# Cross-covariance attention: V loaded eight heads at a time, in 8 KB runs

## The chip, the core and the metric

The kernel runs on one core of one Trainium2 chip. A core has five engines that run side by side, each with its own queue of instructions in program order: TensorE (PE; its weight loads are listed apart as PEld), VectorE (DVE), ScalarE (ACT), GpSimd (POOL) and SyncE (SP), which here does nothing but issue transfers. Sixteen DMA engines move data between HBM and the on-chip memory SBUF; matmuls write into PSUM. The metric is the device time of one execution in microseconds.

## What is computed

For each of 8 batches and 12 heads there are Q, K and V of 512 rows by 64 columns, float32. Q and K are divided by the norm of each of their columns, the 64x64 matrix of their products is put through a softmax along its last axis, and V is multiplied by it:

```python
Q_norm = Q / (np.linalg.norm(Q, axis=-2, keepdims=True) + 1e-10)
K_norm = K / (np.linalg.norm(K, axis=-2, keepdims=True) + 1e-10)
attn = np.einsum('bhnd,bhne->bhde', Q_norm, K_norm)
attn = np.exp(attn - np.max(attn, axis=-1, keepdims=True))
attn = attn / (np.sum(attn, axis=-1, keepdims=True) + 1e-10)
out = np.einsum('bhnd,bhde->bhne', V, attn)
```

Inputs are 37.75 MB and the output 12.58 MB.

## The kernel before

The work is cut into 24 units of 4 heads. A unit's Q, K and V are 512 KB each. Each is loaded into a tile of 128 partitions, 32 partitions to a head, with 16 rows of 64 values (4 KB, one contiguous run) in a partition. The output of a unit is stored with two runs of 2 KB in a partition.

What is done for one unit:

- Q and K are cast to bf16 into one tile, side by side (`cast_q` L80, `cast_k` L83, VectorE). 64 matmuls give each head's 128x128 Gram matrix (`grams` L95). Its diagonal holds the squared norms (`norms` L107, VectorE, and a power on GpSimd, L112), its lower left block K against Q, which ScalarE keeps (`keep_kq` L100), GpSimd scales (L117), TensorE transposes (`logits` L123) and VectorE scales (`scale_q` L127). Then come the exponential (`exps` L131, ScalarE) and the division (`normalise` L135 to L139, VectorE), which writes the softmax into a block-diagonal matrix; a matmul and a ScalarE copy place it a second time (`doubled` L165, L166).
- V is cast to bf16 into `vb`, one half on ScalarE and one on VectorE (`cast_v` L88). TensorE transposes eight blocks of 128x128, each with two rows of V in its columns, into one PSUM tile (`vtrans` L145), and one ScalarE copy brings them to SBUF as `vt` (L148). That copy goes in the order of its source: it reads PSUM contiguously and writes every other bf16 element, so that two blocks lie interleaved.
- `outs` (L176) multiplies the transposed V by the block-diagonal softmax, half a unit in each PSUM tile `po`; copies (L180) bring the result to `so`, and `store` (L76) writes it out.

The order is written out by hand; nothing is reordered. Iteration s of the main loop loads Q and K of unit s+3, computes the Gram matrix of unit s, the logits of s-1, and the outputs of units n0 to n1-1, where n1 = `outs_by(s)` is (s-2)*9//10 and at least 0. So outputs fall behind, and at the end 6 of the 24 units are left. V is loaded up to unit n1+3, cast and transposed up to unit n1; the casts stand at the head of the iteration, ahead of `cast_q(s+1)` on VectorE. On TensorE an iteration runs grams, logits, outs, doubled, vtrans. Stores follow three outputs behind. All transfers are issued from SP's queue in that order, and each issue waits until the transfer eight places earlier has landed.

After the loop the Gram matrices' PSUM is free, and the last units' V goes without the cast: `vtrans_f32` (L159, L160) transposes float32 blocks, two PSUM tiles to a unit, and ScalarE and VectorE copy one each. It runs one unit ahead of `outs`. There `outs` has one of its two copies on each engine.

Of the kernel before, what the change touches and what calls it, by code (L numbers as in the profile page):

```python
# [8 lines left out]
F32 = mybir.dt.float32  # L9
BF16 = mybir.dt.bfloat16  # L10
# [4 lines left out]
D = 64  # L15
HU = 4
NV = 32
R = 16
SV = 2
MV = 64  # L20
TP = 4
# [3 lines left out]
def kernel(  # L25
# [7 lines left out]
    nc = tc.nc  # L33
    B, H, N, _ = Q.shape
    assert N == NV * R and Q.shape[3] == D
    U = B * H // HU

    Qf, Kf, Vf = (x.rearrange("b h n d -> (b h n d)").rearrange("(u p f) -> u p f", p=128, f=R * D) for x in (Q, K, V))
    Of = out.rearrange("b h n d -> (b h n d)").rearrange("(u s p f) -> u p s f", s=SV, p=128, f=TP * 2 * D)

    ctx.enter_context(tc.manual_schedule())

    const = ctx.enter_context(tc.tile_pool(name="const", bufs=1))
    qp = ctx.enter_context(tc.tile_pool(name="qp", bufs=5))
    vp = ctx.enter_context(tc.tile_pool(name="vp", bufs=6))
    vbp = ctx.enter_context(tc.tile_pool(name="vbp", bufs=4))
    qkp = ctx.enter_context(tc.tile_pool(name="qkp", bufs=4))
    vtp = ctx.enter_context(tc.tile_pool(name="vtp", bufs=3))
    sop = ctx.enter_context(tc.tile_pool(name="sop", bufs=10))
# [2 lines left out]
    ps_v = ctx.enter_context(tc.tile_pool(name="ps_v", bufs=1, space=bass.MemoryType.PSUM))  # L52
# [5 lines left out]
    def outs_by(s):  # L58

        return max(0, (s - 2) * 9 // 10)  # L60


    qf, kf, vf, vb, qkb, nsq, rq, kqs, sl, ex, vt, so, kq = ({} for _ in range(13))

    def load_qk(u):
        qf[u] = qp.tile([128, R, D], F32, name="qf")
        kf[u] = qp.tile([128, R, D], F32, name="kf")
        nc.sync.dma_start(out=qf[u].rearrange("p t d -> p (t d)"), in_=Qf[u])
        nc.sync.dma_start(out=kf[u].rearrange("p t d -> p (t d)"), in_=Kf[u])

    def load_v(u):
        vf[u] = vp.tile([128, R * D], F32, name="vf")
        nc.sync.dma_start(out=vf[u], in_=Vf[u])

    def store(u, g=slice(0, SV)):
        nc.sync.dma_start(out=Of[u][:, g], in_=so[u][:, g].rearrange("p s t d -> p s (t d)"))  # L76

    def cast_q(u):
        qkb[u] = qkp.tile([128, R, 2 * D], BF16, name="qkb")
        nc.vector.tensor_copy(qkb[u][:, :, 0:D], qf[u])  # L80
# [1 line left out]
    def cast_k(u):  # L82
        nc.vector.tensor_copy(qkb[u][:, :, D:], kf[u])  # L83

    def cast_v(u):
        w = vb[u] = vbp.tile([128, R // 2, 2 * D], BF16, name="vb")
        for half, copy in ((slice(0, TP), nc.scalar.copy), (slice(TP, None), nc.vector.tensor_copy)):
            copy(w[:, half], vf[u].rearrange("p (t d) -> p t d", d=2 * D)[:, half])  # L88

    def grams(u):  # L90

# [29 lines left out]
    def logits(u):  # L121
        for h in range(HU):
            nc.tensor.transpose(lg[:, h, :], kqs[u][D:, h, :], ident[D:, D:])  # L123

    def scale_q(u):
        s = sl[u] = small.tile([D, HU, D], F32, name="sl")
        nc.vector.tensor_tensor(out=s, in0=lg, in1=rq[u][0:D, :, None].to_broadcast([D, HU, D]), op=ALU.mult)  # L127

    def exps(u):
        e = ex[u] = small.tile([D, HU, D], F32, name="ex")  # L130
        nc.scalar.activation(e, sl[u], AF.Exp)  # L131

    def normalise(u):
        s = small.tile([D, HU], F32, name="esum")
        nc.vector.reduce_sum(out=s, in_=ex[u], axis=AX.X)  # L135
        ri = small.tile([D, HU], F32, name="rinv")
        nc.vector.reciprocal(ri, s)
        a = abuf[u % len(abuf)]
        nc.vector.tensor_tensor(out=a[0:D, :, 0, :], in0=ex[u], in1=ri[:, :, None].to_broadcast([D, HU, D]), op=ALU.mult)  # L139

    def vtrans(u):

        ps = ps_v.tile([128, R // 2, 128], BF16, name="vps")
        for t in range(R // 2):
            nc.tensor.transpose(ps[:, t, :], vb[u][:, t, :], identb)  # L145

        w = vt[u] = vtp.tile([128, TP, 128, 2], BF16, name="vt")
        nc.scalar.copy(w.rearrange("p t c a -> p a t c"), ps.rearrange("p (a t) c -> p a t c", a=2))  # L148

    def vtrans_f32(u):  # L150

        w = vt[u] = vtp.tile([128, TP, 128, 2], BF16, name="vt")
        for i in range(2):
            half = slice(i * TP // 2, (i + 1) * TP // 2)
            ps = ps_t.tile([128, TP // 2, 128, 2], F32, name="vps32")
            for t in range(TP // 2):
                for a in range(2):
                    c = (a * TP + i * TP // 2 + t) * 2 * D
                    nc.tensor.transpose(ps[:, t, :, a], vf[u][:, c:c + 2 * D], ident)  # L159
            both[i](w[:, half], ps)  # L160

    def doubled(u):

        a = abuf[u % len(abuf)]
        nc.tensor.matmul(dup[D:], identb[0:D, 0:D], a[0:D, :, 0, :], tile_position=(0, D))  # L165
        nc.scalar.copy(a[D:, :, 1, :], dup[D:])  # L166

    def outs(u, copies=(nc.scalar.copy, nc.scalar.copy)):
        s = so[u] = sop.tile([128, SV, TP, 2 * D], F32, name="so")
        a = abuf[u % len(abuf)]  # L170
        for g in range(SV):
            po = ps_o.tile([128, TP, 2 * D], F32, name="po")
            for t in range(TP):
                for x in range(2):
                    h = 2 * g + x
                    nc.tensor.matmul(  # L176
                        po[MV * x:MV * (x + 1), t, :], vt[u][:, t, NV * h:NV * (h + 1), :].rearrange("p c a -> p (c a)"),
                        a[:, h].rearrange("p a d -> p (a d)"), tile_position=(0, MV * x),
                    )
            copies[g](s[:, g], po)  # L180
# [11 lines left out]
    ident = const.tile([128, 128], F32, name="ident")  # L192
    make_identity(nc, ident)
    identb = const.tile([128, 128], BF16, name="identb")
# [4 lines left out]
    for i in range(12):  # L199
        a = const.tile([128, HU, 2, D], BF16, name=f"ab{i}")  # L200
# [3 lines left out]
    def on(f, u):  # L204
        if 0 <= u < U:
            f(u)

    on(cast_q, 0)
    on(cast_k, 0)
    on(load_v, 0)  # L210
    on(load_v, 1)
    nv, nst, nt = 2, 0, 0
    for s in range(U):
        n0, n1 = outs_by(s - 1), outs_by(s)
        on(load_qk, s + LOAD_AHEAD)
        while nv < min(U, n1 + 4):
            load_v(nv)
            nv += 1
        while nst < n1 - 3:
            store(nst)  # L220
            nst += 1
        new = range(nt, n1 + 1) if s >= 1 else ()
        for v in new:
            cast_v(v)
        on(cast_q, s + 1)
        on(normalise, s - 2)
        on(grams, s)
        on(norms, s)
        on(keep_kq, s)
        on(scale_k, s)  # L230
        on(logits, s - 1)
        on(scale_q, s - 1)
        on(exps, s - 1)
        on(cast_k, s + 1)
        for v in range(n0, n1):
            outs(v)
        on(doubled, s - 2)
        for v in new:
            vtrans(v)
            nt = v + 1  # L240
# [3 lines left out]
    ps_t = ctx.enter_context(tc.tile_pool(name="ps_t", bufs=4, space=bass.MemoryType.PSUM))  # L244
    both = (nc.scalar.copy, nc.vector.tensor_copy)

    for i, u in enumerate(range(n1, U)):
        on(load_v, u + 4)
        store(u - 3)
        if i == 0:  # L250
            normalise(last - 1)
        if i == 2:
            scale_q(last)
            exps(last)
        if i == 3:
            normalise(last)
        on(vtrans_f32, u + 1)
        if i == 1:
            doubled(last - 1)
        if i == 3:  # L260
            doubled(last)
        outs(u, both)
        if i == 1:
            logits(last)
    for u in range(U - 3, last):
        store(u)
    for g in range(SV):
        store(last, slice(g, g + 1))
# [29 lines left out]
```

## Time and profile before

| what | value |
| --- | --- |
| median of 6 runs | 131.41 us (131.25 to 132.6) |
| the profiled execution's own time | 131.63 us |
| its span, first to last instruction | 129.9 us |
| busy: DVE, ACT, PE, POOL | 98.9, 88.7, 87.3, 70.2 us |
| q1, the queue of all loads and stores | 16912 packets, 50.34 MB |
| transfers: Q, K, V, out | 24, 24, 24 of 512 KB; 23 of 512 KB and 2 of 256 KB |
| issue to landing, Q, K, V, out | 10.2, 10.3, 10.2, 10.0 us median |

The profile is of one execution. A line of the timeline has the start in us from the first instruction, the duration in us, the engine, the line of the kernel, the operation, what it writes and reads, and in brackets the idle time of its engine just before it and what ended it. SPq is SP's queue. A line of a group has how often the instruction ran, then its busy time in us and the mean of one in ns, then the idle time just before it. The chain of waits is followed back from the last instruction, at each step to what released it; its lines have start, duration, engine, tile and line. The row of digits cuts the span into 40 slices, each digit the busy share in tenths.

### The profile page before, as it was taken

What the parts mean: (1) busy time and instruction counts of PE and PEld (TensorE: products, weight loads), DVE (VectorE), ACT (ScalarE), POOL (GpSimd) and SP (SyncE); (2) the same over time, 40 slices, a digit from 0 to 9 for tenths busy, and PEclk for the clock granted to TensorE, in tenths of its full rate; (3) what the DMA queues carried; (4) which work ended last, traced back from release to release, by engine and by line L of the source; (5) the groups of instructions that cost most, each with busy time, mean ns of one, the idle gap of its engine ahead of it and who ended that gap; (6) DMA issues with size and microseconds to landing.
All of it is one profiled execution on the core that took longest, in us unless ns stands there. A gap on an engine that the chain in (4) does not pass through costs nothing.

```text
span 129.9 us, 5436 instructions
## 1 busy us (share of the span) xinstructions
PE 87.3 (67%) x2232; PEld 67.5 (52%) x2232; DVE 98.9 (76%) x366; ACT 88.7 (68%) x158; POOL 70.2 (54%) x68
## 2 busy tenths in 40 slices
PE   0034778389965678775975797684986689697810
PEld 0043566268754456553754585462864477476600
DVE  0774986986996994984898879986879698598720
ACT  3001442529698996994998398999889988986610
POOL 7924466575664782681678447765745684600000
PEclk9999999999999977998699559999599968999985
DMA  4999999999999999999999999999999999999891
GB/s 151 337 416 419 410 405 411 405 405 406 408 406 406 416 413 408 415 409 405 411 406 416 415 409 415 413 413 409 421 404 415 409 410 406 411 399 382 336 383 74
DMA packets 16936, 50.67 MB, mean 390 GB/s; under 512 B 1552, under 2 KB 1552, under 8 KB 16912
## 3 DMA queue, kind: packets, MB, share of 16 engines
q1 hardware_dynamic: 16912, 50.34, 97.7%
q8 instruction: 17, 0.28, 0.8%
q14 instruction: 7, 0.06, 0.1%
HBM read 37.75 MB, written 12.58 MB: 388 GB/s over the span
## 4 chain that ended last, share of the span: by engine, by line
PE 28%; ACT 26%; DMA 14%; issue 11%; DVE 11%; POOL 4%; SPq 1%; ACTq 0%; DVEq 0%; POOLq 0%
DMA qf<-in_Q_dram 14%; PE gram L95 10%; ACT vt L148 9%; ACT so L180 8%; PE po L176 6%; DVE scr L107 6%; PE vps L145 4%; POOL rq L112 3%; PE vps L159 3%; ACT kq L100 3%; ACT ex L131 3%; ACT ab L166 3%; PE lgdup L165 2%; PE lgdup L123 2%; DVE so L180 1%
## 5 line engine op out<-in xcount | busy, mean ns | idle before, releaser
L112 POOL TENSOR_TENSOR rq<-nsq,mhalf 128x4 f32<-128x4 f32 x24 | 47.1, 1965 | 41.1 <-DVE nsq L107 34.8
L95 PE MATMUL gram<-qkb 32*128 32x128 bf16 x1536 | 36.0, 257 | 18.1 <-DVE qkb L83 11.8
L95 PEld LDWEIGHTS <-qkb 32*128 32x128 bf16 x1536 | 29.8, 115 | 26.0 <-DVE qkb L83 16.2
L107 DVE CUSTOM_DVE_ANT_0 scr<-gram,ident 128x128 f32<-128x128 f32 x96 | 22.0, 283 | 13.0 <-PE gram L95 13.0
L100 ACT COPY kq<-gram 64x256 f32<-64x256 f32 x24 | 8.8, 368 | 27.2 <-DVE nsq L107 26.9
L148 ACT COPY vt<-vps 128x1024 bf16<-128x1024 bf16 x19 | 24.7, 1303 | 0.5
L80 DVE CAST qkb<-qf 128x1024 bf16<-128x1024 f32 x24 | 19.7, 822 | 5.2 <-DMA qf<-in_Q_dram 5.1
L180 ACT COPY so<-po 128x512 f32<-128x512 f32 x42 | 22.8, 588 | 1.2 <-PE po L176 0.5
L176 PE MATMUL po<-ab,vt 128*64 128x128 bf16 x384 | 17.4, 236 | 5.0 <-ACT vt L148 3.9
L176 PEld LDWEIGHTS <-vt 128*64 128x64 bf16 x384 | 12.9, 118 | 11.2 <-ACT vt L148 5.2
L117 POOL TENSOR_TENSOR kqs<-kq,rq 64x256 f32<-64x256 f32 x24 | 16.5, 686 | 1.9
L83 DVE CAST qkb<-kf 128x1024 bf16<-128x1024 f32 x24 | 16.2, 675 | 0.0
L123 PE MATMUL lgdup<-ident,kqs 64*64 64x64 f32 x96 | 11.7, 251 | 6.2 <-POOL kqs L117 4.3
L145 PE MATMUL vps<-identb,vb 128*128 128x128 bf16 x152 | 14.6, 253 | 0.0
L145 PEld LDWEIGHTS <-vb 128*128 128x128 bf16 x152 | 10.7, 113 | 5.5 <-ACT kq L100 3.7
L88 ACT CAST vb<-vf 128x512 bf16<-128x512 f32 x19 | 11.8, 619 | 1.3 <-DMA vf<-in_V_dram 1.3
L165 PE MATMUL lgdup<-ab,identb 64*64 64x256 bf16 x24 | 7.5, 312 | 6.8 <-DVE sl L127 5.9
L123 PEld LDWEIGHTS lgdup<-ident,kqs 64*64 64x64 f32 x96 | 7.1, 123 | 8.9 <-POOL kqs L117 6.8
L131 ACT ACTIVATE ex<-sl 64x256 f32<-64x256 f32 x24 | 10.0, 417 | 2.1 <-DVE sl L127 1.5
L127 DVE TENSOR_TENSOR sl<-lgdup,rq 64x256 f32<-64x256 f32 x24 | 9.9, 411 | 1.9 <-POOL rq L112 1.2
L139 DVE TENSOR_TENSOR ab<-ex,rinv 64x256 bf16<-64x256 f32 x24 | 10.3, 430 | 0.8
L135 DVE TENSOR_REDUCE esum<-ex 64x4 f32<-64x256 f32 x24 | 9.7, 403 | 1.0 <-ACT ex L131 1.0
(20 smaller groups left out, 59.9 us busy)
## 6 DMA issues: line engine op xcount, KB each, us to landing
qf<-in_Q_dram SPq DMA_DIRECT2D x24, 512.0 KB, 10.2
kf<-in_K_dram SPq DMA_DIRECT2D x24, 512.0 KB, 10.3
vf<-in_V_dram SPq DMA_DIRECT2D x24, 512.0 KB, 10.2
out_dram<-so SPq DMA_DIRECT2D x23, 512.0 KB, 10.0
out_dram<-so SPq DMA_DIRECT2D x2, 256.0 KB, 4.4
```

The costliest lines, as they stand in the source:

```text
L80: nc.vector.tensor_copy(qkb[u][:, :, 0:D], qf[u])
L83: nc.vector.tensor_copy(qkb[u][:, :, D:], kf[u])
L95: nc.tensor.matmul(gbuf[:, h, 0:2 * D], x, x, start=(t == 0), stop=(t == R - 1), tile_position=(NV * h, 0))
L107: nc.vector.tensor_tensor_reduce(out=scr, in0=gbuf[:, h, 0:2 * D], in1=ident, scale=1.0, scalar=1e-20, op0=ALU.mult, op1=ALU.add, accum_ou ...
L112: nc.gpsimd.tensor_tensor(out=r, in0=n2, in1=mhalf, op=ALU.pow)
L117: nc.gpsimd.tensor_tensor(out=kk[D:], in0=kq[u][D:], in1=rq[u][D:, :, None].to_broadcast([D, HU, D]), op=ALU.mult,)
L123: nc.tensor.transpose(lg[:, h, :], kqs[u][D:, h, :], ident[D:, D:])
L131: nc.scalar.activation(e, sl[u], AF.Exp)
L145: nc.tensor.transpose(ps[:, t, :], vb[u][:, t, :], identb)
L148: nc.scalar.copy(w.rearrange("p t c a -> p a t c"), ps.rearrange("p (a t) c -> p a t c", a=2))
L176: nc.tensor.matmul(po[MV * x:MV * (x + 1), t, :], vt[u][:, t, NV * h:NV * (h + 1), :].rearrange("p c a -> p (c a)"), a[:, h].rearrange("p ...
L180: copies[g](s[:, g], po)
```

## The change

V is loaded as 12 pairs of units. A pair has 8 heads, 16 partitions to a head, and in a partition 32 rows of 64 values: one run of 8 KB, 1 MB in a transfer. The tiles `vf`, `vb` and `vt` hold pairs; their pools have 4, 3 and 3 buffers where there were 6, 4 and 3 of half the size.

Rows of V in a partition are numbered a, t and a half: a in 4, t in 4, two rows in a block of 128 columns. A unit's step now works on two of the four t, for all partitions and all a: `cast_v(v)` casts one t on ScalarE and one on VectorE (four runs of 128 values each), `vtrans(v)` transposes eight blocks and copies them into `vt` in the order of the destination, whose innermost index is a: four elements that lie 512 bytes apart in PSUM become four neighbours. `vtrans_f32` does the same with float32, its transposes writing PSUM at a step of 4 elements where it was 2.

`outs(u)` takes half of the columns of the pair's `vt`, and all t, so it needs both steps of its pair. Casts and transposes therefore go up to unit n1+1 in the main loop, and two units ahead of `outs` after it. Pairs are loaded while their number is below (n1+5)//2 in the loop and (u+6)//2 after it.

```diff
-    vp = ctx.enter_context(tc.tile_pool(name="vp", bufs=6))
-    vbp = ctx.enter_context(tc.tile_pool(name="vbp", bufs=4))
+    vp = ctx.enter_context(tc.tile_pool(name="vp", bufs=4))
+    vbp = ctx.enter_context(tc.tile_pool(name="vbp", bufs=3))
...
-    def load_v(u):
-        vf[u] = vp.tile([128, R * D], F32, name="vf")
-        nc.sync.dma_start(out=vf[u], in_=Vf[u])
+    def load_v(w):
+        vf[w] = vp.tile([128, 2 * R * D], F32, name="vf")
+        nc.sync.dma_start(out=vf[w], in_=Vf[w])
...
-    def cast_v(u):
-        w = vb[u] = vbp.tile([128, R // 2, 2 * D], BF16, name="vb")
-        for half, copy in ((slice(0, TP), nc.scalar.copy), (slice(TP, None), nc.vector.tensor_copy)):
-            copy(w[:, half], vf[u].rearrange("p (t d) -> p t d", d=2 * D)[:, half])
+    def cast_v(v):
+
+        w, i = divmod(v, 2)
+        if i == 0:
+            vb[w] = vbp.tile([128, A, TP, 2 * D], BF16, name="vb")
+        x = vf[w].rearrange("p (a t d) -> p a t d", a=A, d=2 * D)
+        for t, copy in ((2 * i, nc.scalar.copy), (2 * i + 1, nc.vector.tensor_copy)):
+            copy(vb[w][:, :, t], x[:, :, t])
...
-        w = vt[u] = vtp.tile([128, TP, 128, 2], BF16, name="vt")
-        nc.scalar.copy(w.rearrange("p t c a -> p a t c"), ps.rearrange("p (a t) c -> p a t c", a=2))
...
+    def vtrans(v):
+
+        w, i = divmod(v, 2)
+        ps = ps_v.tile([128, A, 2, 128], BF16, name="vps")
+        for t in range(2):
+            for a in range(A):
+                nc.tensor.transpose(ps[:, a, t, :], vb[w][:, a, 2 * i + t, :], identb)
+
+        if i == 0:
+            vt[w] = vtp.tile([128, TP, 128, A], BF16, name="vt")
+        nc.scalar.copy(vt[w][:, 2 * i:2 * i + 2], ps.rearrange("p a t c -> p t c a"))
+
+    def vtrans_f32(v):
+
+        w, i = divmod(v, 2)
+        if i == 0:
+            vt[w] = vtp.tile([128, TP, 128, A], BF16, name="vt")
+        for t in range(2 * i, 2 * i + 2):
+            ps = ps_t.tile([128, 128, A], F32, name="vps32")
+            for a in range(A):
+                c = (a * TP + t) * 2 * D
+                nc.tensor.transpose(ps[:, :, a], vf[w][:, c:c + 2 * D], ident)
+            both[t % 2](vt[w][:, t], ps)
...
+        v = vt[u // 2][:, :, u % 2 * 64:(u % 2 + 1) * 64]
...
-                        po[MV * x:MV * (x + 1), t, :], vt[u][:, t, NV * h:NV * (h + 1), :].rearrange("p c a -> p (c a)"),
+                        po[MV * x:MV * (x + 1), t, :], v[:, t, NP * h:NP * (h + 1), :].rearrange("p c a -> p (c a)"),
...
-    on(load_v, 0)
-    on(load_v, 1)
-    nv, nst, nt = 2, 0, 0
+    load_v(0)
+    nv, nst, nt = 1, 0, 0
...
-        while nv < min(U, n1 + 4):
+        while nv < min(U, n1 + 5) // 2:
...
-        new = range(nt, n1 + 1) if s >= 1 else ()
+        new = range(nt, n1 + 2) if s >= 1 else ()
...
-        on(load_v, u + 4)
+        while nv < min(U, u + 6) // 2:
+            load_v(nv)
+            nv += 1
...
-        on(vtrans_f32, u + 1)
+        on(vtrans_f32, u + 2)
```

More of the change, by code (lines that the diff above doesn't have):

```diff
@@ L18 @@
 R = 16
+HV = 8
+NP = 16
+A = 4
 SV = 2
@@ L36 @@
     U = B * H // HU
-    Qf, Kf, Vf = (x.rearrange("b h n d -> (b h n d)").rearrange("(u p f) -> u p f", p=128, f=R * D) for x in (Q, K, V))
+    Qf, Kf = (x.rearrange("b h n d -> (b h n d)").rearrange("(u p f) -> u p f", p=128, f=R * D) for x in (Q, K))
+    Vf = V.rearrange("b h n d -> (b h n d)").rearrange("(w p f) -> w p f", p=128, f=2 * R * D)
     Of = out.rearrange("b h n d -> (b h n d)").rearrange("(u s p f) -> u p s f", s=SV, p=128, f=TP * 2 * D)
@@ L139, in normalise @@
         nc.vector.tensor_tensor(out=a[0:D, :, 0, :], in0=ex[u], in1=ri[:, :, None].to_broadcast([D, HU, D]), op=ALU.mult)
[L141 to L145, printed above, removed]
-        w = vt[u] = vtp.tile([128, TP, 128, 2], BF16, name="vt")
[L148 to L160, printed above, removed]
+    def vtrans(v):
[17 more added lines that the diff above has]
+            both[t % 2](vt[w][:, t], ps)
     def doubled(u):
```

## The prediction

> **What bounds the kernel now.** I read the page first, then the chain of waits, then the two queues that meet near the end. The page's slices and its queue table say that the DMA engines are full from the second slice to the last but one:
>
> ```profile
> span 129.9 us, 5436 instructions
> DMA  4999999999999999999999999999999999999891
> GB/s 151 337 416 419 410 405 411 405 405 406 408 406 406 416 413 408 415 409 405 411 406 416 415 409 415 413 413 409 421 404 415 409 410 406 411 399 382 336 383 74
> DMA packets 16936, 50.67 MB, mean 390 GB/s; under 512 B 1552, under 2 KB 1552, under 8 KB 16912
> q1 hardware_dynamic: 16912, 50.34, 97.7%
> ```
>
> So bytes alone nearly fill the span. But the chain of waits, in order of time, leaves the DMA at 21.27 us and never returns to it. Its ends:
>
> ```profile
> 10.55 10.70 DMA qf<-in_Q_dram
> 21.27 1.09 DVE qkb L80
> ...
> 110.70 0.38 ACT ab L166
> 111.09 0.94 ACT vt L148
> ...
> 121.90 0.36 PE po L176 x8
> 122.29 0.59 ACT so L180
> 122.93 0.79 PE po L176 x16
> 123.74 0.69 DVE so L180
> ```
>
> Both are limits, and close to each other: compute writes its last output tile at 124.43, the last store is issued at 124.45 and lands at 128.91 (its semaphore, in the trace). From here on "lands" is the DMA's sixteenth semaphore step. The first load, with nothing ahead of it, is issued at 0.74 and lands at 4.04, 3.3 us, and a 512 KB transfer takes 1.28 of the queue; so the last stores still stand in the DMA queue, and compute has less than 2 us to spare. A change that speeds the DMA and delays compute has to be weighed at both.
>
> **The DMA's gain.** The trace's packet records of q1 have medians of 159 ns for 4096 bytes (9216 packets, all loads), 84 ns for 2048 (6144, stores) and 9 ns for the 4-byte semaphore writes (1552). 75 ns for 2 KB more leaves 9 ns fixed in each packet, so 8 KB is estimated at 309. V has 3072 packets, which become 1536: 1536 x 9 ns = 13.8 us of engine time. Twelve transfers fewer save 12 x 16 x 9 ns = 1.7 us. Over 16 engines that is **0.97 us**, 0.081 per 1 MB pair. [...] I take the measured 9. The low bound is 0.1 (8 KB costs two 4 KB packets); no row shows 8 KB in this queue.
>
> **What waits for V.** With 8 heads in 128 partitions, one unit's four heads lie in half the partitions, and each output needs both half-transposes of its pair. So the cast and the transpose of unit v move one iteration earlier (n1+2 for n1+1), while pair v/2 is issued where V of its even unit was, and lands a transfer later: a lead of three iterations becomes two. SP has eight transfers in flight, so the issue eight places later tells when a transfer has landed. SP's queue, around the last V that the main loop casts:
>
> ```profile
> 92.38 0.33 SPq L73 DMA_DIRECT2D vf<-in_V_dram  x1
> 93.69 0.39 SPq L76 DMA_DIRECT2D out_dram<-so  x1
> ...
> 103.24 0.33 SPq L73 DMA_DIRECT2D vf<-in_V_dram  x1
> 104.53 0.39 SPq L76 DMA_DIRECT2D out_dram<-so  x1
> ```
>
> V18 is issued at 92.38 and lands at 103.16, store 11 behind it at 104.47. Pair 9 (V18, V19) fills both places: 104.47 less ten pairs' 0.81 is **103.66**. VectorE casts V18 in iteration s=21 of the new code, at the head of the iteration, where now V17 is cast:
>
> ```profile
> 100.34 0.41 DVE L88 CAST vb<-vf 128x512 bf16<-128x512 f32 x1
> 100.67 0.68 DVE L80 CAST qkb<-qf 128x1024 bf16<-128x1024 f32 x1
> 101.27 0.40 DVE L135 TENSOR_REDUCE esum<-ex 64x4 f32<-64x256 f32 x1
> 103.35 0.29 DVE L107 CUSTOM_DVE_ANT_0 scr<-gram,ident 128x128 f32<-128x128 f32 x1 [1.02 <-PE gram L95]
> ```
>
> So VectorE would stand for 3.3 us at 100.34. Queued behind it are cast_q(22), normalise(19) and norms(21). The cast takes until 104.07, cast_q to 104.7, normalise to 105.68: norms(21) starts there and not at 103.35, **2.33 us late**, since 1.02 of the stall falls into a wait that was there. Norms(21) holds scale_q(20), which holds the doubling matmul (PE waits for sl at 104.66 today), which holds, in PE's order, the transpose and gram(22), and so norms(22), keep_kq(22) and everything to the end. ScalarE's half of the cast stood at 103.44 and loses 0.2. I see no slack in this chain: from 103.35 it is the chain of waits itself. The same count for earlier pairs: pair 7 lands at 82.75 against a cast wanted at 82.8, pair 8 at 92.89 against 92.0. At the start, pair 0 lands at 14.30 where V0 landed at 13.10, and iteration 1 casts two units: VectorE loses 1.2 + 0.4, of which 1.02 fits into its wait for qf at 21.27 (cast_k(3) ends 1.9 later, cast_q(4) 0.9). That 0.9 is still under the 3.3 of iteration 21, which swallows it.
>
> **The tail.** Twenty instead of nineteen units go through the main loop, so the last transposing step before outs(22) falls away. Up to outs(21) the order is today's. Let L be the lateness there, 2.33. Store 21 is issued at 121.68 now, so at 121.68 + L; then 3.3 to land, 1.27 for store 22 and 1.28 for the two halves of 23: last landing **127.53 + L**. Here compute follows fast enough without the transposes: copies of outs(22) and (23) 0.9 apart. By the DMA alone the end is 128.91 - 0.97 = 127.94. The later one holds: 127.53 + 2.33 = 129.86, **0.95 later** than now. A store's latency on an empty queue is not in the trace; taking it 0.5 off the load's either way moves the end by 0.5.
>
> **The ScalarE copy into vt.** The rows:
>
> ```profile
> L100 ACT COPY kq<-gram 64x256 f32<-64x256 f32 x24 | 8.8, 368 | 27.2 <-DVE nsq L107 26.9
> L148 ACT COPY vt<-vps 128x1024 bf16<-128x1024 bf16 x19 | 24.7, 1303 | 0.5
> L180 ACT COPY so<-po 128x512 f32<-128x512 f32 x42 | 22.8, 588 | 1.2 <-PE po L176 0.5
> ```
>
> From 368 to 588 ns for 256 elements more, 1024 contiguous ones would be 588 + 440 = 1028; today's copy, contiguous in PSUM and stepping 4 bytes in SBUF, takes 275 more. The new one writes in order and steps 512 bytes through PSUM for each element. If the step in SBUF was the price, it falls to 1028. [...] so I [...] take the nearest row, 1303, no change. At 1028 L falls by 0.27 (one copy lies between norms(21) and outs(21)). At 1.9, 18 copies of the main loop add 10.8 us to a ScalarE that is idle for 10.9 of the 80 us from 30 to 110 (its busy time in the eight stretches of ten us: 8.82, 9.31, 8.42, 8.33, 6.67, 9.71, 8.67, 9.16): with half of that idle time staying, L is 5.4.
>
> **At nothing:** the casts' four runs of 128 (L100 reads four runs and L166 one, 368 and 367 ns); the f32 transposes' step of 16 for 8 bytes in PSUM [...]; twelve SP issues fewer, 0.33 us each, on a queue that waits for landings; VectorE and ScalarE copies of the tail, same size. Q and K behind a pair land 0.4 to 1.8 later, when their casts are later still. The vt ring, three pairs, frees earlier than it is needed.
>
> **Sum.** 131.63 is the profiled execution's time, 129.9 its span: 131.63 + 0.95 = 132.58. It stands 0.22 above the median of 131.41, so on medians **132.3**, 0.7% slower. About 0.5% is what a measurement of this kernel can tell from no change (130.75 to 132.07).
>
> **Rivals and chances.**
> - *The V wait decides, copy 1.03 to 1.4 us*: 131.7 to 132.9, chance 0.45, a quarter of it within 0.5%. For it: 103.66 against 100.34 rests on the queue's order and the landings, not on a guess of a duration.
> - *The PSUM step slows the copy*: 1.5 to 1.95 us; at L = 5.4 the end is 132.93, 135.4 in all; 133.5 to 138. [...] 0.25.
> - *The change doesn't do what it says*: 8 KB runs move as two 4 KB packets. Gain 0.1, pair 9 lands at 104.4, L = 3.1: 133.1. Chance 0.1. For it: no 8 KB packet in this queue; against: other queues have packets of 8192 bytes and more.
> - *VectorE's and ScalarE's casts of one pair get ordered by a wait*, as they write alternate runs of one tile: VectorE's would wait for ScalarE's, 3 us later in each iteration (100.34, 103.44); over 137. 0.05.
> - *The other side*: the delay is taken up before outs(21), by the even units alone having to wait for the newest vt (PE waits for vt at 99.50 now, 0.68), and by a copy of 1.03. The point is L = 0.7 for 0.5% faster, 1.38 for no change; at L up to 0.41 the DMA's 0.97 is paid in full: 130.4. Against: VectorE's three instructions behind the V cast have 1.02 of slack. 0.15, half of it within 0.5%.
>
> Slower 0.33 + 0.25 + 0.1 + 0.05 = 0.73; same 0.12 + 0.07 = 0.19; faster 0.08. Range 130.9, in the last case's middle, to 136.5, in the slow copy's; the likeliest alone 131.7 to 132.9.
>
> **What would show it.** q1 with 1536 packets of 8 KB and some 309 ns each; VectorE's V cast of iteration 21 waiting about 3 us for vf, at 103.7; norms(21) near 105.7; outs(21) stored near 124.0; a gap between the DMA's last stores; the vt copy near 1.3. I am wrong if the vt copy is above 1.5, if pair 9 lands before 102.7, or if outs(21) is stored before 123.

## The result, and the profile after

The changed kernel takes 132.44 us in the median of 35 executions (131.18 to 135.67), the kernel before 131.33 (70 executions, 130.78 to 132.92). Their ratio is 1.004, with a 95% interval of 1.0022 to 1.0059: slower by 0.4%, 0.53 us. The comparison leaves out executions over 1.5% above the fastest of their kernel, 13 of the 35 and 1 of the 70, which is why the ratio is below that of the medians, and the profiles of the changed kernel are all of such executions.

There are three profiles of the changed kernel. Up to 105 us they agree, but for transfers that land a microsecond later in one of them; in the last 25 us they differ, and this part is read apart. The page of the first, the same lines as before:

```profile
span 133.1 us, 5388 instructions
DMA  4999999999999999999999999999999999944775
GB/s 156 340 412 427 425 401 409 406 424 400 415 411 404 428 403 407 428 402 414 414 414 411 414 424 402 413 424 406 412 424 400 427 409 416 374 186 182 294 262 211
DMA packets 15208, 50.67 MB, mean 381 GB/s; under 512 B 1360, under 2 KB 1360, under 8 KB 13648
q1 hardware_dynamic: 15184, 50.34, 94.7%
```

1536 of V's packets now have 8 KB, 1728 packets in all are gone. But the DMA is no longer full at the end: its last six slices were 9, 9, 9, 8, 9, 1 before and are 9, 4, 4, 7, 7, 5. The store of the last halves tells the same. It is issued with 4.4 us to landing before the change, in a queue, and now with 3.1 us, on an empty one:

```profile
vf<-in_V_dram SPq DMA_DIRECT2D x12, 1024.0 KB, 12.5
out_dram<-so SPq DMA_DIRECT2D x2, 256.0 KB, 3.1
```

The chain of waits of the changed kernel shows where compute lost its place. Its columns are start, duration, engine, tile and line; L96 is now `cast_v`, L115 `norms`, L170 `vtrans_f32`:

```profile
79.24 11.54 DMA kf<-in_K_dram
90.80 12.57 DMA vf<-in_V_dram
103.39 0.43 DVE vb L96
103.81 0.60 DVE qkb L84
...
105.32 0.28 DVE scr L115
...
106.62 0.37 PE lgdup L176
...
107.95 1.83 PE gram L103 x64
...
116.22 1.90 PE vps L170 x8
...
128.19 0.69 DVE so L192
```

Before, the chain left the DMA at 21.27. Now it comes back to it at 79.24 and waits for pair 9 until 103.36, its landing; from VectorE's cast of V18 it is compute again to the end. The timeline of VectorE has the wait itself:

```profile
100.64 0.67 DVE L87 CAST qkb<-kf 128x1024 bf16<-128x1024 f32 x1
103.39 0.43 DVE L96 CAST vb<-vf 128x512 bf16<-128x512 f32 x1 [2.07 <-DMA vf<-in_V_dram]
```

Norms(21) starts at 105.32 where it started at 103.35. In two further profiles of the changed kernel pair 9 landed at 103.45 and 104.33; the first has norms(21) at 105.40.

The groups show what else changed. The copy into vt is cheaper, 1012 ns in the mean where it was 1303, and there are 20:

```profile
L108 ACT COPY kq<-gram 64x256 f32<-64x256 f32 x24 | 8.8, 368 | 31.3 <-DVE nsq L115 31.2
L192 ACT COPY so<-po 128x512 f32<-128x512 f32 x42 | 22.8, 588 | 2.3 <-PE po L188 1.8
L159 ACT COPY vt<-vps 128x1024 bf16<-128x1024 bf16 x20 | 20.2, 1012 | 1.8 <-PE vps L155 1.4
```

Three stretches of the tail, first of the kernel before, then of the changed one. The third number from the end is the granted clock of TensorE, the last two are the DMA's share and GB/s:

```profile
105.00:110.00 5.00, 4.88 (x109) 3.84 (x111) 4.45 (x17) 4.59 (x9) 3.21 (x3) 0.66 1.03 405
110.00:115.00 5.00, 3.83 (x98) 3.08 (x99) 3.54 (x17) 4.67 (x9) 2.71 (x4) 1.00 1.04 409
115.00:120.00 5.00, 4.29 (x58) 3.40 (x57) 4.43 (x10) 3.49 (x7) 0.00 (x0) 1.00 1.01 389
```

```profile
105.00:110.00 5.00, 3.38 (x76) 2.68 (x76) 4.19 (x17) 3.58 (x7) 3.21 (x2) 0.60 1.03 414
110.00:115.00 5.00, 5.00 (x97) 3.87 (x96) 3.15 (x18) 3.41 (x7) 2.26 (x2) 0.50 1.03 409
115.00:120.00 5.00, 4.20 (x32) 3.45 (x32) 3.30 (x12) 2.33 (x6) 1.62 (x2) 0.54 0.58 224
```

In this execution TensorE had half its clock just then, from 106.0 to 119.6 us: the group of eight f32 transposes at 116.2 took 1.97 us on its timeline, where the last two such groups, at 121.48 and 123.07 with the clock at 1.00, took 1.09. Store 21 was issued at 126.56, 4.88 later than before: 1.97 from the wait, and 2.9 gathered between norms(21) and outs(21). This second part goes with the length of the half clock, as the profiles set side by side under the last experiment show, and is not taken as part of the 0.4%.

### The profile page after: what moved, and what is told of

The parts are those of the page before. It is cut to its first block, busy times and chain, and to the rows that moved or that the text cites. A ratio compares the mean times of both kernels' runs of the same rounds, so it can differ in the third digit from the quotient of the medians.

```text
span 133.1 us, 5388 instructions
## 1 busy us (share of the span) xinstructions
PE 91.6 (69%) x2232; PEld 71.4 (54%) x2232; DVE 98.3 (74%) x366; ACT 84.8 (64%) x159; POOL 69.3 (52%) x68
## 4 chain that ended last, share of the span: by engine, by line
PE 35%; DMA 26%; DVE 20%; issue 6%; POOL 4%; ACT 3%; SPq 2%; DVEq 0%; POOLq 0%; ACTq 0%
DMA vf<-in_V_dram 18%; PE gram L103 15%; DMA kf<-in_K_dram 9%; DVE scr L115 8%; PE vps L155 6%; PE po L188 5%; POOL rq L120 3%; PE vps L170 3%; PE lgdup L176 3%; DVE sl L135 3%; PE lgdup L131 2%; DVE qkb L87 2%; DVE qkb L84 2%; DVE vb L96 1%; DVE ab L147 1%
## 5 line engine op out<-in xcount | busy, mean ns | idle before, releaser
L120 POOL TENSOR_TENSOR rq<-nsq,mhalf 128x4 f32<-128x4 f32 x24 | 48.0, 2000 | 45.5 <-DVE nsq L115 40.6
L103 PE MATMUL gram<-qkb 32*128 32x128 bf16 x1536 | 37.5, 264 | 18.0 <-DVE qkb L87 11.0
L103 PEld LDWEIGHTS <-qkb 32*128 32x128 bf16 x1536 | 31.3, 118 | 24.9 <-DVE qkb L87 14.1
L115 DVE CUSTOM_DVE_ANT_0 scr<-gram,ident 128x128 f32<-128x128 f32 x96 | 22.1, 284 | 15.4 <-PE gram L103 15.3
L159 ACT COPY vt<-vps 128x1024 bf16<-128x1024 bf16 x20 | 20.2, 1012 | 1.8 <-PE vps L155 1.4
L188 PE MATMUL po<-ab,vt 128*64 128x128 bf16 x384 | 18.6, 244 | 1.8 <-ACT so L192 0.9
L155 PEld LDWEIGHTS <-vb 128*128 128x128 bf16 x160 | 11.9, 116 | 12.6 <-ACT kq L108 6.5
L155 PE MATMUL vps<-identb,vb 128*128 128x128 bf16 x160 | 16.2, 261 | 2.9 <-ACT vt L159 2.4
L188 PEld LDWEIGHTS <-vt 128*64 128x64 bf16 x384 | 13.8, 123 | 6.2 <-issue 4.1
L125 POOL TENSOR_TENSOR kqs<-kq,rq 64x256 f32<-64x256 f32 x24 | 14.7, 612 | 1.9
L96 ACT CAST vb<-vf 128x512 bf16<-128x512 f32 x20 | 12.3, 621 | 2.5 <-DMA vf<-in_V_dram 2.5
L96 DVE CAST vb<-vf 128x512 bf16<-128x512 f32 x20 | 8.3, 419 | 4.6 <-DMA vf<-in_V_dram 4.6
## 6 DMA issues: line engine op xcount, KB each, us to landing
vf<-in_V_dram SPq DMA_DIRECT2D x12, 1024.0 KB, 12.5
```

Source lines behind the costliest of these rows:

```text
L96: copy(vb[w][:, :, t], x[:, :, t])
L103: nc.tensor.matmul(gbuf[:, h, 0:2 * D], x, x, start=(t == 0), stop=(t == R - 1), tile_position=(NV * h, 0))
L115: nc.vector.tensor_tensor_reduce(out=scr, in0=gbuf[:, h, 0:2 * D], in1=ident, scale=1.0, scalar=1e-20, op0=ALU.mult, op1=ALU.add, accum_ou ...
L120: nc.gpsimd.tensor_tensor(out=r, in0=n2, in1=mhalf, op=ALU.pow)
L125: nc.gpsimd.tensor_tensor(out=kk[D:], in0=kq[u][D:], in1=rq[u][D:, :, None].to_broadcast([D, HU, D]), op=ALU.mult,)
L155: nc.tensor.transpose(ps[:, a, t, :], vb[w][:, a, 2 * i + t, :], identb)
```

## The experiments

All medians are in us, with the ratio to the kernel before on the same chip and its 95% interval.

| kernel | median | ratio |
| --- | --- | --- |
| changed, once more | 132.0 | 1.0002 (0.9976 to 1.0028) |
| before, V cast one iteration earlier | 132.97 | 1.0066 (1.0039 to 1.0093) |
| changed, pairs in 4 KB runs | 134.06 | 1.0164 (1.0115 to 1.0214) |
| changed, pair 0 cast later | 133.01 | 1.0085 (1.005 to 1.0119) |
| before, stores later | 131.8 | 1.0031 (1.0014 to 1.0048) |
| changed, stores later | 131.34 | 0.9983 (0.996 to 1.0006) |
| before, three moves | 131.69 | 1.002 (1.0001 to 1.0038) |
| changed, three moves | 131.13 | 0.9978 (0.9956 to 1.0) |
| changed, three moves, stores later still | 131.03 | 0.996 (0.9936 to 0.9983) |
| before, vt copy in order of destination | 131.69 | 1.0018 (1.0 to 1.0036) |
| changed, vt copy in order of source | 147.24 | 1.1205 (1.1161 to 1.1249) |

Two theories stood against each other. A: the wait for V, which the shorter lead makes, takes compute's slack at the end. B: the pair layout's compute is slower by itself.

**The changed kernel once more**, nothing edited:

> The changed kernel once more, for a profile to set beside the others. Theory A (the wait for V): VectorE's cast of V18 waits for pair 9 until 103.3 to 103.7 us, norms(21) starts near 105.3 to 105.7, where it starts at 103.35 before the change; the stores from number 18 on find the DMA queue empty and land about 2.9 us after their issue. The time is 131.4 to 132.6, and depends on the clock that TensorE is granted after 105 us, since nothing stands between compute and the end any more. Theory B (the pair layout's compute is slower by itself): cast, transposes and copies take longer per unit than before, and the lateness grows over the whole loop instead of appearing in one iteration.

The wait was 1.95 us at 103.47, norms(21) at 105.40, store 21 at 124.98: 3.3 late, 2.05 of it there at norms(21). The copy into vt and the casts of V on ScalarE and VectorE take 1012, 621 and 419 ns in the mean; before the change they took 1303, 619 and 437. That speaks for A. The ratio came out at 1.0002, so that the two measurements together say between no loss and 0.6%.

**The short lead alone.** The kernel before, its casts and transposes one iteration earlier, V in single units and 4 KB runs:

```diff
-        new = range(nt, n1 + 1) if s >= 1 else ()
+        new = range(nt, n1 + 2) if s >= 1 else ()
...
-        on(vtrans_f32, u + 1)
+        on(vtrans_f32, u + 2)
```

(and 4 buffers for vt instead of 3)

> The kernel before with its casts and transposes of V one iteration earlier, as the change has them, and one buffer more for vt; V comes unit by unit in 4 KB runs as before. Theory A: V18 is wanted at 100.3 and lands at 103.2, norms(21) is about 1.8 late, the tail has one transposing step less; the end is the later of the DMA's 128.9 and about 127.1 + 1.8: 131.3 to 131.9, 0 to 0.5% slower, with a wider spread of the runs than the kernel before. Theory B: nothing waits and the time is 131.3 or less.

It is 0.66% slower, a little more than A expected, and B is out as the whole cause: no pair, no 8 KB run and no new copy is in this kernel. Its waits of VectorE for V, total, times and longest:

```profile
DVE vb L88 <- DMA vf<-in_V_dram: 6.9, 8, 1.1
```

and the one of iteration 21 on VectorE's timeline, with norms(21) behind it:

```profile
102.10 0.89 DVE L88 CAST vb<-vf 128x512 bf16<-128x512 f32 x1 [0.95 <-DMA vf<-in_V_dram]
...
104.50 0.27 DVE L107 CUSTOM_DVE_ANT_0 scr<-gram,ident 128x128 f32<-128x128 f32 x1
```

Not one wait but eight: one at 13.3 us, and then one in each iteration from 76.9 us on. Compute no longer runs behind the loads with some distance, but at their heels. Norms(21) is 1.15 late and store 21 2.73, with another wait of 1.06 for V19 between them, and the last store finds an empty queue (3.1 us to landing). The executions spread from 131.64 to 135.81, much as the changed kernel's do, so that spread does not need pairs either.

**The 8 KB runs taken away.** The changed kernel, each pair in two transfers:

```diff
-        nc.sync.dma_start(out=vf[w], in_=Vf[w])
+        for c in range(2):
+            cols = slice(c * R * D, (c + 1) * R * D)
+            nc.sync.dma_start(out=vf[w][:, cols], in_=Vf[w][:, cols])
```

> The changed kernel with each pair loaded as two transfers of 4 KB runs, the halves of every partition's 8 KB; all else as the change has it. Theory A (each packet has a fixed part of 9 ns): 1536 packets of 8 KB become 3072 of 4 KB at 159 ns, the queue loses 0.97 us in all and 0.8 up to pair 9, which lands near 104.2; VectorE waits that much longer in iteration 21, and the time is 0.5 to 1.0 us above the changed kernel's: 132.3 to 133.3. Rival (the length of the run does not matter): as the changed kernel, 131.4 to 132.4.

The second half of pair 9 landed at 104.22, as worked out, and VectorE's cast of V18 started at 104.31. The loss against the changed kernel is 1.2 to 1.6%, more than the 0.4 to 0.75% expected. The two profiles in which the half clock lasts about as long (6.8 us), this one and that of the changed kernel once more, are apart by what the landings say: pair 9 by 0.77 us, norms(21) by 0.84, store 21 by 0.83, the whole by 0.74 (134.04 and 133.3). Why the medians, here of 6 executions, are further apart is not settled. The edit also makes twice as many transfers of V, so that it does not tell the length of the runs from the number of transfers.

**The early delay.** Two casts in iteration 1 delay cast_q(4) to 23.1 us, from 21.27. The changed kernel, pair 0 cast in iterations 2 and 3:

```diff
-        new = range(nt, n1 + 2) if s >= 1 else ()
+        new = range(nt, min(n1 + 2, s - 1))
```

> The changed kernel with the two casts and transposes of pair 0 in iterations 2 and 3 instead of both in iteration 1. Theory A, as in the prediction (the early delay is swallowed by iteration 21): cast_q(4) starts near 21.3 to 21.8 instead of 23.3, the wait for V in iteration 21 grows from 2.1-2.5 to 3 us or more, and the time stays within 0.3% of the changed kernel's. Rival (the early delay is what makes it slower): 131.0 or less.

Cast_q(4) went back to 20.7, and nothing was won. The time went into waits for V, which VectorE's timeline shows for pairs 7, 8 and 9:

```profile
82.77 0.43 DVE L96 CAST vb<-vf 128x512 bf16<-128x512 f32 x1 [2.50 <-DMA vf<-in_V_dram]
...
92.75 0.43 DVE L96 CAST vb<-vf 128x512 bf16<-128x512 f32 x1 [1.67 <-DMA vf<-in_V_dram]
...
103.28 0.43 DVE L96 CAST vb<-vf 128x512 bf16<-128x512 f32 x1 [2.63 <-DMA vf<-in_V_dram]
```

So pair 9's landing holds iteration 21 wherever compute comes from, and the rival, that the early delay makes the loss, falls. The measured 1.0085 is above the 0.3% that A allowed. Its profile has clocks of 0.57, 0.50 and 0.56 in the three stretches from 105 to 120; beside the changed kernel's first profile, with 0.60, 0.50 and 0.54, norms(21) starts 0.12 us earlier and the whole takes 0.16 less (134.72 and 134.88). So at a like clock the two are the same, and why the medians differ is open.

**Loads earlier in the queue.** The same edit in both kernels puts stores behind loads:

```diff
-        while nst < n1 - 3:
+        while nst < n1 - 5:
...
-        store(u - 3)
+        store(u - 5)
...
-    for u in range(U - 3, last):
+    for u in range(U - 5, last):
```

> The changed kernel with stores two outputs further behind, so that the last five outputs before the end wait in SBUF and every load from unit 12 on stands up to two transfers (2.56 us) earlier in the queue; the bytes are the same. Theory A (the wait for V): pair 9 lands near 100.8, the cast of V18 waits for less than 0.7 us, compute ends at 124.0 to 124.7, and the DMA, full until the end, sets it at 127.9 to 128.4: 130.4 to 130.9 us, 0.4% to 0.7% below the kernel before. Theory B (compute of the pair layout): 131.5 to 132.5 as the changed kernel, since compute is not helped.

> The kernel before with the same stores two outputs further behind. Both theories: 131.1 to 131.6, no difference to the kernel before, since its DMA queue is full to the end either way and its bytes and packets are the same. If it is faster by 0.5% or more, the later stores are worth something by themselves and the gain of the changed kernel with late stores is not the wait for V.

In the changed kernel pair 9 landed at 101.17 and VectorE's wait shrank to 0.32. Against 1.0002 and 1.004 the ratio is 0.9983: some of the gain is there, not the 0.4 to 0.7% expected, and its interval takes in no change. Compute was still last (3.3 us from the last issue to landing). It probably carries the early delay, which the wait for pair 9 no longer covers: norms(21) starts at 104.44 here, and at 102.69 in the next kernel, which takes that delay away too. The kernel before gets 0.3% slower by the same edit, against both expectations. In its profile the last store was issued at 125.92 instead of 124.45, though norms(21) started 0.83 us earlier than before. What came later came behind it, where the half clock lasted from 109.2 to 116.0 instead of from 104.9 to 108.4:

```profile
110.00:115.00 5.00, 4.20 (x65) 3.26 (x59) 2.44 (x13) 3.04 (x5) 1.62 (x2) 0.50 1.04 407
```

Whether the other executions had the same is not known. The run does show that later stores are no gain by themselves.

**All three moves.** Later stores, pair 0 cast in iterations 2 and 3, and

```diff
-    load_v(0)
-    nv, nst, nt = 1, 0, 0
+    nv, nst, nt = 0, 0, 0
...
-        while nv < min(U, n1 + 5) // 2:
+        while nv < (min(U, n1 + 5) // 2 if s else 1):
```

so that pairs 0 and 1 stand behind Q and K of units 3 and 4. The counterpart for the kernel before loads V0 and V1, then V2 and V3 at these places and casts V0 in iteration 2.

> The changed kernel with three moves: stores two outputs further behind, casts of pair 0 in iterations 2 and 3, pairs 0 and 1 loaded behind Q and K of units 3 and 4. Theory A: no engine waits for V near the end, compute has an earlier start by 1 to 2 us, the last stores stand in a full queue again, and the DMA's 0.97 us is paid out: last landing 127.9 to 128.3, 130.4 to 130.8 us. Rival (compute of the pair layout, or the granted clock, sets the end): 131.2 or more.

> The kernel before with the same three moves (V0 to V3 behind Q and K of units 3 and 4, V0 cast in iteration 2, stores two further behind). Theory A: its queue holds 0.97 us more and is full to the end, so 131.1 to 131.5, no faster than the kernel before. Rival (the moves are worth the gain by themselves, the 8 KB runs nothing): as low as the changed kernel with the three moves.

The last landing was 127.96 in the changed kernel (127.94 was worked out for a full queue) and 128.72 in the other, 0.76 apart. The times are 131.13 and 131.69, both above what was expected, but the order of the two is as A has it: the kernel before gains nothing by the moves, and with them the changed kernel, with its 8 KB runs, is 0.4% below it. VectorE's cast of V18 still waited 1.8 us for pair 9.

**Stores later still**, seven outputs behind and 12 buffers for them instead of 10:

```diff
-        while nst < n1 - 5:
+        while nst < n1 - 7:
...
-        store(u - 5)
+        store(u - 7)
```

> The changed kernel with the three moves, and stores two further behind still (seven outputs behind the newest where the change has three), with two more buffers for them. In the profile with three moves the cast of V18 still waits 1.8 us for pair 9, and the last store stands only 1.1 us longer than on an empty queue. Theory A: pair 9 lands near 98.2, that wait is gone, the last store stands 5 us or more in a full queue, and a low granted clock at the end no longer reaches the time: 130.5 to 130.9 us, and fewer runs above 131.5. Rival (nothing left to gain by order): 131.1 as with three moves.

This version is faster than the kernel before, by 0.4% (0.17 to 0.64). Its page, and its only wait of VectorE for V:

```profile
span 129.2 us, 5382 instructions
DMA  4999999999999999999999999999999999999981
out_dram<-so SPq DMA_DIRECT2D x2, 256.0 KB, 6.3
```

```profile
DVE vb L96 <- DMA vf<-in_V_dram: 0.4, 1, 0.4
```

The queue is full to the end and the last store stands in it for 6.3 us. The median is 0.13 above the expected range. Compute has more than 3 us to spare here (6.3 less the 3.1 of an empty queue), so what is left above 130.5 is in the queue, not in compute. In this execution the half clock began at 122.2, behind the last issue (121.78), so the profile does not show what the version makes of a low clock in the tail; of its 12 executions one is above 131.5.

**The copy into vt**, in both directions:

```diff
-        nc.scalar.copy(vt[w][:, 2 * i:2 * i + 2], ps.rearrange("p a t c -> p t c a"))
+        nc.scalar.copy(vt[w][:, 2 * i:2 * i + 2].rearrange("p t c a -> p a t c"), ps)
```

> The changed kernel with its vt copy in the order of the source: PSUM read contiguously, every fourth bf16 element of SBUF written (8 bytes apart). If the step in SBUF is what costs, the copy takes 1.3 us or more (the copy with steps of 4 bytes took 1303 ns), 0.3 to 0.6 above the 1012 of the order of destination; one copy lies in the chain between iteration 21 and the end, so the time is 0.3 to 1.0 us above the changed kernel's. If instead the step in PSUM costs something, it takes less than 1012.

```diff
-        nc.scalar.copy(w.rearrange("p t c a -> p a t c"), ps.rearrange("p (a t) c -> p a t c", a=2))
+        nc.scalar.copy(w, ps.rearrange("p (a t) c -> p t c a", a=2))
```

> The kernel before with its vt copy in the order of the destination, two elements side by side that lie 1 KB apart in PSUM: near 1012 ns instead of 1303 by the same reason. ScalarE is 5 us less busy, but the DMA queue is full to the end, so the time stays at 131.0 to 131.5. Rival (ScalarE's copy is what paces the kernel): 130.8 or less.

The group of the changed kernel in order of source, then that of the kernel before in order of destination:

```profile
L159 ACT COPY vt<-vps 128x1024 bf16<-128x1024 bf16 x20 | 48.9, 2446 | 1.6 <-PE vps L155 1.1
```

```profile
L148 ACT COPY vt<-vps 128x1024 bf16<-128x1024 bf16 x19 | 19.2, 1012 | 0.5
```

In order of destination the copy took 1012 ns whether two or four blocks are interleaved; in order of source 1303 with steps of 4 bytes in SBUF and 2446 with steps of 8. The direction was expected, the 2446 was not, nor that it makes the kernel 12% slower: 20 x 1.43 = 28.7 us more of ScalarE, of which 15.6 end up in the span against the kernel before. The kernel before gains nothing from the cheap copy (1.0018), though ScalarE is 4.9 us less busy: its queue is full to the end, and its last store waits 5.3 us to land instead of 4.4.

**One more profile of the changed kernel**, for the clock:

> The changed kernel for one more profile, to set the granted clock behind iteration 21 beside the time. Theory A: norms(21) starts at 105.2 to 105.7 again, whatever the time; if the clock row shows full clock from 105 to 118 us, outs(21) is stored near 123.4 (1.7 late) and the time is 130.9 to 131.6; with half clock there, near 125 to 126.6 and 132.5 to 135. Rival: the time does not go with the clock in these slices.

The two executions took 132.1 and 135.86. The profile is of the second: pair 9 landed at 104.33, a microsecond late, and norms(21) started at 106.28, so that its expected 105.2 to 105.7 was missed with the landing; the clock from 105 to 120 was 0.69, 0.50 and 0.50. Beside it stand 134.88 (0.60, 0.50, 0.54) and 133.3 (0.78, 0.54, 1.00). What lies between 135.86 and 134.88 is the later landing (norms(21) 0.96 apart); the half clock is as long in both. No profile of the changed kernel has full clock there, so that side of the expectation stays open. But the kernel with stores later still has it, with the same compute behind norms(21), and the time from there to the issue of store 21 can be set beside the clock:

| profiles | half clock in this time | norms(21) to store 21 |
| --- | --- | --- |
| before | 3.4 us, from 104.9 | 18.33 us |
| changed, stores later still | none | 18.15 |
| changed, stores later; changed, three moves | 6.2 to 6.8, from 104.4 and 103.1 | 18.41; 18.76 |
| changed, once more; changed, pairs in 4 KB runs | 6.8, from 107.8 and 108.7 | 19.58; 19.57 |
| changed, first and third profile; changed, pair 0 cast later | 13.7, from 105.7 to 106.9 | 21.24, 21.23; 21.17 |

The ends of this time in the kernel with stores later still, then store 21 of the changed kernel's first profile, which had norms(21) at 105.32:

```profile
101.27 0.29 DVE L115 CUSTOM_DVE_ANT_0 scr<-gram,ident 128x128 f32<-128x128 f32 x1 [0.29 <-PE gram L103]
119.42 0.37 SPq L80 DMA_DIRECT2D out_dram<-so  x1
```

```profile
126.56 0.37 SPq L80 DMA_DIRECT2D out_dram<-so  x1
```

So of the lateness at store 21 the wait makes some 2 us, and the half clock up to 3 more, by its length and by where it lies. What it costs outside of the profiled executions is not shown.

## Why the prediction was right, and where not

The forecast was 132.3 us, 0.7% slower, with 130.9 to 136.5 around it. The comparison gives 131.33 x 1.004 = 131.86, the median of all executions 132.44. Direction and range held. The loss is smaller than forecast and, at 0.22% to 0.59%, lies for the most part in the band that the prediction called no change, to which it gave 0.19; measured once more it was none (1.0002). The medians of all executions are 0.8% and 0.4% apart.

- **The DMA's gain: right.** The 8 KB packets have a median of 309 ns, as worked out from 159 and 84. The means are 313.4 for 8 KB and 162.7 for 4 KB, so 12.0 ns saved for each pair of packets instead of 9. It was paid out only where compute kept up: 0.76 us of last landing between the two kernels with three moves, of 0.97.
- **The wait for V: right.** Pair 9 was put at 103.66 and landed at 103.36; norms(21) was put at 105.68 and started at 105.32, 1.97 late and not 2.33. VectorE stood for 2.07 and not 3.3, since it came later: the early delay was worked out as 0.9 at cast_q(4) and was 1.9. The prediction had counted VectorE's part alone (and its 1.2 + 0.4 less 1.02 would be 0.6). What it left out is TensorE, where the second transpose of iteration 1 waits for the copy of the first, since their PSUM pool has one buffer, and gram(2) stands behind it, 3.06 us later than the 16.34 of before (its lines are below). That iteration 21 swallows it is shown by the kernel with pair 0 cast later. That the short lead alone costs time is shown by the kernel before with that lead. TensorE in iteration 1 of the changed kernel:

```profile
18.46 1.01 PE L155 MATMUL vps<-identb,vb 128*128 128x128 bf16 x8 [2.43 <-ACT vt L159]
19.40 1.89 PE L103 MATMUL gram<-qkb 32*128 32x128 bf16 x64
```

- **The copy into vt: wrong value.** Of the two ends, 1028 and 1900 ns, the nearest row was taken, 1303; it measures 1012. The low end's reading, that the step in SBUF is the price and the step in PSUM none, is what the copies in both directions show: 1012 ns with steps of 512 bytes or 1 KB in PSUM, beside the 1028 estimated for no step at all, and 1303 and 2446 with steps of 4 and 8 bytes in SBUF. The high end doubles the 880 ns that the prediction's rows give for 1024 elements (588 - 368 for every 256); no trace had shown a doubling, and no run shows it. To give it less weight was right, to stay at 1303 was not. It is 0.29 us less in L.
- **The tail: form right, latency wrong.** A store on an empty queue was put at 3.3 us by the first load; stores 18 to 21 landed 2.8 to 3.0 after their issue. With the landings of the changed kernel, store 21 needs 5.49 to the end of all (129.38 - 126.56 = 2.82, then 1.36, 0.66, 0.65), not 5.85.
- **The sum.** With the measured terms L at full clock is 1.97 - 0.29 = 1.68, and the last landing 121.68 + 1.68 + 5.49 = 128.85, where it was 128.91: no change at all, and not 0.95 later. (By the 18.15 us from norms(21) to store 21 at full clock, where it was 18.33 before with 3.4 us of half clock, what comes off L is 0.18 and the end is 128.96; no change either.) So the mis-sized terms are the latency of a store (0.36), the copy (0.29) and the wait (0.36), all on the same side. The 0.53 us that were measured come on top of this sum, so that the direction came out as forecast is in part luck: the sum with its terms put right forecasts no loss. A half clock in the tail, which now reaches the time, would do it: the time from norms(21) to store 21 is 1.4 us longer with 6.8 us of it from 108 on than at full clock, and 3.1 longer with 13.7, and the prediction had no term for it. How much of it there is in an execution near the median no profile of the changed kernel shows, so as the source of the 0.53 it is argued, not shown.
- **Rivals.** Runs of 8 KB moving as two packets, and the casts of a pair ordered by a wait, are out: 1536 packets of 8 KB, and VectorE's cast of V18 starts 0.03 after the landing. The slow copy is out for this change and true for the other order. The case on the other side, the delay taken up before outs(21), came near: L at full clock is at its point of no change (1.38 by the old latency, 1.74 with 5.49). What brought it there was the copy and the store's latency, not the even units.

## What to carry to other kernels

DMA and compute end within 2 us of each other here, and the cheaper transfer was worth nothing until compute had the time to use it: an estimated 0.97 us of DMA came to a loss of 0.4% with a lead of two iterations, and to a gain of 0.4% once stores stood further behind the loads and the loads that compute needs first came first. The larger transfers lengthened the way from issue to landing, in the median from 10.2 to 12.5 us for V; count for each consumer when the whole transfer lands, by the queue's order, and compare it with the time at which the consumer comes now. ScalarE's interleaving copy from PSUM was cheaper in the order of its destination in both kernels here (1012 ns against 1303 and 2446), and its cost is worth a measurement before the layout is chosen.

## What was not expected of the hardware

- ScalarE's copy of 1024 bf16 elements from PSUM to SBUF: 1012 ns with contiguous writes and reads 512 bytes (or 1 KB) apart, 1303 with contiguous reads and writes 4 bytes apart, 2446 with writes 8 bytes apart.
- The clock granted to TensorE fell to 0.50 for 13.7 us in the tail of the changed kernel in two of three profiles, and for 6.8 in the third; before, for 3.4. It stayed there while TensorE had no idle time: 5.00 us busy of the 5.00 from 110 to 115 us in the first of them. It fell in every profiled execution here (a mean of 0.83 to 0.92 over the span). In the changed kernel with three moves it was 0.51 from 105 to 110 us, and the last landing did not follow: 127.96, 0.02 from the full queue's 127.94.
